# Two attentions keep program order on ScalarE and VectorE, gates close two pieces later, a memory tile is loaded apart from its square

## The chip, the cores and the metric

The kernel runs on one core of a Trainium2 chip. Five engines work side by side: TensorE (matmuls into PSUM banks; PE in the profile, its weight loads PEld), VectorE (DVE), ScalarE (ACT), GpSimd (POOL) and SyncE (SP), which here only issues DMAs. ScalarE and GpSimd issue DMAs too. Each engine takes its instructions from its own queue in a fixed order and waits on semaphores for the others. The metric is the device time of one execution in microseconds, the median of several runs.

## The reference

One layer of a decoder trunk, 1024 tokens of width 1024. Cut to what matters:

```python
h = rms_norm(x, norm1_g)
proj = h @ w_in                      # all branches' inputs and the gates
p_rwkv, p_sb, q_mem, gate_logits = split(proj)
y_a = rwkv7_branch(p_rwkv, ...)      # recurrence with a delta-rule state
y_b = stick_breaking_branch(p_sb)    # 8 heads of 64, causal, sigmoid weights and a reverse cumulative product
y_m = memory_branch(q_mem, mem, ...) # 4 heads of 128, softmax over 256 memory tokens
gates = sigmoid(gate_logits)         # 3 branches x 1024
x = x + sum_b(gates_b * (branch_b @ w_branch_b)) @ w_out
x = x + conv_ffn(rms_norm(x, norm2_g))
```

Everything is float32. A matmul that must be exact enough is made of three passes on TensorE's faster format: each operand is split into a high part and the rest.

## The kernel before, in words

The program is traced by Python in one order, and a planner then lays each engine's queue. The planner keeps its own clock: an instruction that by that clock has its inputs and its buffer is put into the queue, and one traced earlier that hasn't is passed by. So a queue's order can differ from the traced order. `pinned(ins)` (while `self.pin` is set) takes that freedom from one instruction: it comes behind the instruction traced just before it on the same engine, whatever that is. An instruction between two pinned ones that isn't pinned itself may still be put further ahead. Before the change all matmuls and transposes are pinned, and on VectorE the scans of the first attention and the triangular inverse.

TensorE's time is filled by weaving. A main generator (the first attention, then the second, then the recurrence) is run step by step, and after each step `weave` runs so many pieces of a filler, which is a stream of items. An item is mostly a projection: `proj_item` splits the weights (`split_raw`: a ScalarE copy, L80, and a GpSimd subtraction, L81; the split for an item is traced one item ahead), then does eight pieces k = 0 to 7 of six matmuls each into two PSUM banks (of the four with the tag `mm`), and then calls a `fin` that empties the banks. Extra work is hung on pieces by hooks.

- A gate item's `fin` copies the banks out (L745, ScalarE), multiplies by the row norms (L746, VectorE) and leaves a closure in `open_gates`. `close_gates`, called behind piece k = 2 of the next projection item, runs it: the sigmoid (L749) and a store of the gate to DRAM (L751, ScalarE's DMA queue). The gate's tile has the tag `w4`, of which there are three buffers; other items put their raw tiles and squares there too.
- First attention (`sb_attn`): 64 units of one head and 128 queries. `front` makes scores on TensorE and their sigmoid (L838, ScalarE); `weigh` scans (L844, VectorE, pinned); `mid`, two units later, transposes on TensorE (L105) and copies out (L856, ScalarE); `back`, for two units together, makes the weighted sums on TensorE, and then copies the heads out (L879) and stores them (L882, ScalarE's DMA queue). Scores and transposes share the four banks with the tag `g`. During it the fillers are the next heads' q and k projections, gates, and the memory's keys and values.
- Memory (`mem_kv`): `prep`, hung on piece 0 of one gate item and on piece 2 of another, loads 1024 columns of the memory tile (L909, SyncE's queue), squares it (L910) and splits it in four (L914 ScalarE, L915 VectorE). `ss` then sums the squares on TensorE.
- Second attention (`mem_attn`): eight units. `front` makes scores, their maximum (L1053, VectorE), a bias from it and the q norm's factor (L1056, VectorE; the factor comes from GpSimd, L697), exponentials (L1059, ScalarE), a reciprocal and a scaling (L1063, L1065); `mid` transposes and copies (L1074); `back` makes the sums and copies them out (L1084). The q projections are filler items; their `fin` is L1021 and L1022 on ScalarE and L1023 on VectorE.

The stage of the recurrence (`stage2`, about 800 to 1060 us) follows in the same manner, and then the output projection and the feed-forward network.

Of the kernel before, what the change touches and what calls it, by code (L numbers as in the profile page):

```python
# [11 lines left out]
F32 = mybir.dt.float32  # L12
F32R = mybir.dt.float32r
BF16 = mybir.dt.bfloat16
AF = mybir.ActivationFunctionType
ALU = mybir.AluOpType
AX = mybir.AxisListType
# [32 lines left out]
class Trunk:  # L50
# [649 lines left out]
    def proj_item(self, src, fin, hook={}):  # L700
        w = self.split_w(src)
        yield
        out = [self.ps("mm"), self.ps("mm")]
        for k in range(8):
            ks = slice(k * 128, (k + 1) * 128)
            self.mm3(out, [a[:, ks] for a in w], self.xin(k), k == 0, k == 7)
            if k == 2:
                self.close_gates()
            if k in hook:
                hook[k]()  # L710
            if k < 7:
                yield
        fin(out)
        yield
# [24 lines left out]
    def gate_item(self, b, d, hook={}, keep=None):  # L739
        nc = self.nc  # L740

        def fin(pp):
            g = self.t4()
            for h in range(2):
                nc.scalar.activation(g[:, h * 512 : (h + 1) * 512], pp[h], AF.Copy)  # L745
            nc.vector.tensor_tensor(g, g, self.rbc, ALU.mult)  # L746

            def close():
                nc.scalar.activation(g, g, AF.Sigmoid)  # L749
                if keep is None:  # L750
                    nc.scalar.dma_start(self.gsd[b, d], g)  # L751
                else:
                    keep["g", d] = g

            self.open_gates.append(close)

        return self.proj_item(self.I["w_in"][30 + b * 8 + d], fin, hook)
# [62 lines left out]
    def sb_attn(self, qk, need):  # L820
        nc = self.nc
        units = [(p, half, h2, half * 4 + bb) for p in range(4) for h2 in range(2) for half in range(2) for bb in range(4)]
        st = {}

        def front(u):
            p, half, h2, b = units[u]
            need(f"sb{p}")
            S, K, KL, nf = qk[p]
            W = (b + 1) * 128
            ts = slice(b * 128, (b + 1) * 128)  # L830
            sn = self.t4("at", n=1024)
            for w0 in range(0, W, 512):
                w1 = min(w0 + 512, W)
                pz = self.ps("g")
                self.mmul(pz[:, : w1 - w0], S[h2][:, ts], K[h2][:, w0:w1], start=True, stop=False)
                self.mmul(pz[:, : w1 - w0], S[h2][:, ts], KL[h2][:, w0:w1], start=False, stop=True)
                i = 2 * b + h2
                nc.scalar.activation(sn[:, w0:w1], pz[:, : w1 - w0], AF.Sigmoid, scale=nf[:, i : i + 1])  # L838
            st[u] = sn

        def weigh(u):
# [4 lines left out]
        def mid(u):  # L846
            b = units[u][3]
            W = (b + 1) * 128
            at, sn = self.t4("at"), st[u]
            st[u] = at  # L850
            for w0 in range(0, W, 512):
                w1 = min(w0 + 512, W)
                pt = self.ps("g")
                for o in range(w0, w1, 128):
                    self.transpose(pt[:, o - w0 : o - w0 + 128], sn[:, o : o + 128])
                nc.scalar.activation(at[:, w0:w1], pt[:, : w1 - w0], AF.Copy)  # L856

        def back(u):
            p, half, h2, b = units[u]
# [41 lines left out]
    def mem_kv(self):  # L901
        nc = self.nc
        mhi, mlo, sqs, st = [], [], [], {}

        def prep():
            i = len(sqs)
            raw, sq = self.t4(), self.t4()
            hi, lo = self.t4("qk", F32R), self.t4("qk", F32R)
            nc.sync.dma_start(raw, self.I["memT"][:, i * 1024 : (i + 1) * 1024])  # L909
            nc.scalar.activation(sq, raw, AF.Square)  # L910
            for kk in range(4):
                ks = slice(kk * 256, (kk + 1) * 256)
                g = self.par("memg", i * 4 + kk)
                nc.scalar.activation(hi[:, ks], raw[:, ks], AF.Copy, scale=g)  # L914
                nc.vector.scalar_tensor_tensor(lo[:, ks], raw[:, ks], g, hi[:, ks].bitcast(F32), ALU.mult, ALU.subtract)  # L915
            mhi.append(hi)
            mlo.append(lo)
            sqs.append(sq)
# [54 lines left out]
            self.mk = sq, kr, *st["r"]  # L973
            yield

        return prep, ss, [mv(i) for i in range(4)], [mk(h) for h in range(4)]

    def mem_kss(self):
        nc = self.nc
# [32 lines left out]
    def mem_q(self, h, out, hook):  # L1012
        nc = self.nc
        st = []

        def fin(pp):
            sq = self.t4()
            qhi, qlo = self.t4("qk", F32R), self.t4("qk", F32R)
            for i in range(2):
                hs = slice(i * 512, (i + 1) * 512)  # L1020
                nc.scalar.activation(qhi[:, hs], pp[i], AF.Copy, scale=self.par("memq"))  # L1021
                nc.scalar.activation(sq[:, hs], pp[i], AF.Square)  # L1022
                nc.vector.scalar_tensor_tensor(qlo[:, hs], pp[i], self.par("memq"), qhi[:, hs].bitcast(F32), ALU.mult, ALU.subtract)  # L1023
            st.extend((sq, qhi, qlo))

        def ss():
            sq, qhi, qlo = st
            pst = self.ps("g")
            for j in range(8):
                self.colsum(pst[:, j : j + 1], sq[:, j * 128 : (j + 1) * 128], self.ones[:, 0:1])  # L1030
            out.extend((qhi, qlo, self.head_norm(pst, 1, 128, 128 ** -0.5)))

        return self.proj_item(self.I["w_in"][26 + h], fin, hook), ss

    def mem_attn(self, mq, need):
        nc = self.nc
# [3 lines left out]
        def front(v):  # L1040
            h, i = units[v]
            need(f"mq{h}")
            qhi, qlo, f = mq[h]
            e = self.t4("at")
            sm = self.small("sm", [128, 4])
            for b2 in range(2):
                pz = self.ps("g")
                for u in range(2):
                    bs = slice((i * 4 + b2 * 2 + u) * 128, (i * 4 + b2 * 2 + u + 1) * 128)
                    self.mm3([pz[:, u * 256 : (u + 1) * 256]], [qhi[:, bs], qlo[:, bs]],  # L1050
                             [[kx[:, h * 256 : (h + 1) * 256]] for kx in self.kx], True, True)
                mxt = self.small("mxt", [128, 2])
                nc.vector.tensor_reduce(mxt, pz.rearrange("p (u m) -> p u m", u=2), AX.X, ALU.max)  # L1053
                fs = slice(i * 4 + b2 * 2, i * 4 + b2 * 2 + 2)
                nb = self.small("nb", [128, 2])
                nc.vector.scalar_tensor_tensor(nb, mxt, -1.0, f[:, fs], ALU.mult, ALU.mult)  # L1056
                for u in range(2):
                    o = (b2 * 2 + u) * 256
                    nc.scalar.activation(  # L1059
                        e[:, o : o + 256], pz[:, u * 256 : (u + 1) * 256], AF.Exp, bias=nb[:, u : u + 1],  # L1060
                        scale=f[:, fs.start + u : fs.start + u + 1], accum_out=sm[:, b2 * 2 + u : b2 * 2 + u + 1])
            rc = self.small("rc", [128, 4])
            nc.vector.reciprocal(rc, sm)  # L1063
            for b in range(4):
                nc.vector.tensor_scalar(e[:, b * 256 : (b + 1) * 256], e[:, b * 256 : (b + 1) * 256], rc[:, b : b + 1], None, ALU.mult)  # L1065
            es[v] = e

        def mid(v):
            e, pT = es[v], self.t4("at")
            for j in range(2):  # L1070
                pt = self.ps("g")
                for b in range(4):
                    self.transpose(pt[:, b * 128 : (b + 1) * 128], e[:, b * 256 + j * 128 : b * 256 + (j + 1) * 128])
                nc.scalar.activation(pT[:, j * 512 : (j + 1) * 512], pt, AF.Copy)  # L1074
            es[v] = pT

        def back(v):
            h, i = units[v]
            pT = es.pop(v)
            y = pT[:, 0:512]  # L1080
            py = self.ps("mm")
            for j in range(2):
                self.mmul(py, self.vm[:, j * 512 + h * 128 : j * 512 + (h + 1) * 128], pT[:, j * 512 : (j + 1) * 512], start=(j == 0), stop=(j == 1))
            nc.scalar.activation(y, py, AF.Copy)  # L1084
            nc.scalar.dma_start(self.yd[2, h, :, i * 512 : (i + 1) * 512], y)

        for s in range(len(units) + 4):
# [644 lines left out]
    def run(self):  # L1732
        nc, tc = self.nc, self.tc
# [26 lines left out]
        gate = lambda hook={}: self.gate_item(*gq.pop(0), hook)  # L1760
# [5 lines left out]
        mqi = [None] * 4  # L1766
        for h in range(4):
            mqi[h] = self.mem_q(h, mq[h], {2: mqi[h - 1][1], 4: mark(f"mq{h - 1}")} if h > 1 else {})
        items += [gate({0: prep}), gate(), gate({2: prep}), mss, *mv, *mk, mqi[0][0], mark("kv")]
        items += [self.mem_kss, gate({1: mqi[0][1]}), self.mem_kbc, mqi[1][0], mark("mq0")]  # L1770
        items += [mqi[2][0], mqi[3][0], gate({2: mqi[3][1], 4: mark("mq3")}), gate(), mark("mem")]
        ld1, br1 = self.branch(1, True)
# [114 lines left out]
```

## Time and profile before

| | us |
|---|---|
| median of 3 runs | 1866.93 |
| lowest, highest | 1861.88, 1868.17 |
| profiled execution | 1870.84 |
| its span | 1869.1 |
| first attention (ScalarE's first and last L838 to L879) | about 342 to 661 |
| second attention (its first maximum, its last store) | about 703 to 792 |

The page gives busy times by engine; the timeline gives instructions in order of time with, in brackets, how long the engine had been idle before and what ended the idle time. Names are tiles: `at<-g,nf` is written to a tile `at` from a bank `g` and a factor `nf`. L80, L105 and L112 are helpers (weight split, transpose, matmul), so their rows are told apart by their tiles: `mm<-xhi,wh` is a piece of a projection, `g<-qk,qk` scores of the first attention, `mm<-at,A` its weighted sums, `g<-kon,at` transposes, `g<-A,qk` scores of the second attention.

### The profile page before, as it was taken

How to read it: one execution, taken by the hardware profiler on the slowest of the kernel's cores; microseconds unless marked ns; L12 is line 12 of the kernel's file. 1: busy time of each engine (PE TensorE's matmuls, PEld its weight loads, DVE VectorE, ACT ScalarE, POOL GpSimd, SP SyncE). 2: the span in 40 equal slices, each digit the busy share in tenths (PEclk: the TensorE clock that was granted, in tenths of full speed). 3: DMA queues.
4: the chain of work that ended last, by engine and by line, in shares of the span. 5: the costliest groups of instructions: out<-in, count | busy, mean ns of one | idle time of the engine just before them, and what ended most of it. 6: DMA issues, size and time to landing. Idle time of an engine off the chain costs nothing. (4 is left out here: it accounts for less than half of the span.)

```text
span 1869.1 us, 27410 instructions
## 1 busy us (share of the span) xinstructions
PE 1801.6 (96%) x10468; PEld 1454.2 (78%) x10468; DVE 1169.7 (63%) x1654; ACT 884.8 (47%) x1667; POOL 785.7 (42%) x449
## 2 busy tenths in 40 slices
PE   8999999999999999999989999989999999999999
PEld 6777778878787787787767778767888888878877
DVE  5656665998887413333423673376777677785596
ACT  5443343565566535534446443454444444544333
POOL 2322343322222352122233352468676777644454
PEclk9999999999999999999899999999999999999999
DMA  4255465111122441557664472222333232486475
GB/s 177 57 169 180 158 208 177 51 61 43 40 63 65 121 128 40 171 207 260 231 218 170 157 260 91 102 79 95 114 107 108 85 119 97 134 303 221 141 235 193
DMA packets 120614, 263.39 MB, mean 141 GB/s; under 512 B 28314, under 2 KB 40858, under 8 KB 120355
## 3 DMA queue, kind: packets, MB, share of 16 engines
q1 hardware_dynamic: 82722, 194.76, 32.2%
q10 hardware_dynamic: 33984, 54.27, 7.9%
q0 software_dynamic: 3776, 12.62, 2.1%
q8 instruction: 82, 1.34, 0.3%
q14 instruction: 50, 0.40, 0.1%
HBM read 180.04 MB, written 81.53 MB: 140 GB/s over the span
## 5 line engine op out<-in xcount | busy, mean ns | idle before, releaser
L81 POOL TENSOR_TENSOR wl<-wr,wh 128x1024 fp32r<-128x1024 f32 x77 | 195.6, 2541 | 490.0 <-ACT wh L80 479.8
L112 PE MATMUL mm<-xhi,wh 128*128 128x512 f32 x784 | 267.8, 422 | 9.2 <-ACT xhi L179 7.4
L112 PE MATMUL mm<-xlo,wh 128*128 128x512 f32 x784 | 249.1, 400 | 0.8 <-DVE xlo L180 0.8
L112 PE MATMUL mm<-xhi,wl 128*128 128x512 f32 x784 | 246.2, 396 | 0.2 <-POOL wl L81 0.2
L112 PEld LDWEIGHTS mm<-xlo,wh 128*128 128x128 f32 x784 | 151.1, 193 | 35.4 <-DVE xlo L180 1.5
L112 PEld LDWEIGHTS mm<-xhi,wl 128*128 128x128 f32 x784 | 150.2, 192 | 34.6 <-POOL wl L81 0.6
L112 PEld LDWEIGHTS mm<-xhi,wh 128*128 128x128 f32 x784 | 139.7, 194 | 39.8 <-issue 9.1
L80 ACT ACTIVATE wh<-wr 128x1024 fp32r<-128x1024 f32 x77 | 81.4, 1057 | 146.2 <-PE mm L112 86.1
L112 PE MATMUL mm<-dw,da 128*128 128x512 f32 x528 | 121.6, 390 | 2.3 <-DVE da L1627 2.1
L112 PE MATMUL mm<-BT,l 128*128 128x512 f32 x504 | 118.0, 389 | 0.6 <-POOL l L1374 0.6
L112 PEld LDWEIGHTS mm<-dw,da 128*128 128x128 f32 x528 | 98.8, 188 | 24.4 <-DVE da L1627 3.4
L1628 POOL TENSOR_TENSOR dw<-draw,dw 128x512 fp32r<-128x512 f32 x55 | 81.3, 1487 | 83.5 <-ACT dw L1626 82.1
L844 DVE TENSOR_TENSOR_SCAN at<-at,at 128x128 f32<-128x128 f32 (+3 forms) x64 | 91.1, 1427 | 35.3 <-ACT at L838 35.2
L112 PEld LDWEIGHTS mm<-BT,l 128*128 128x128 f32 x504 | 94.5, 188 | 20.6 <-POOL l L1374 1.0
L112 PE MATMUL mm<-BT,wh 128*128 128x512 f32 x352 | 108.9, 390 | 0.7 <-DVE u L1426 0.7
L112 PE MATMUL mm<-B,wh 128*128 128x512 f32 x352 | 108.5, 389 | 0.0
L1627 DVE TENSOR_TENSOR da<-draw,da 128x512 fp32r<-128x512 f32 x77 | 65.7, 863 | 58.9 <-ACT da L1625 58.3
L112 PE MATMUL g<-dw,da 128*128 128x512 f32 x396 | 90.8, 390 | 2.1 <-POOL dw L1628 1.1
L1374 POOL TENSOR_TENSOR l<-it,l 128x1024 fp32r<-128x1024 f32 x21 | 50.8, 2419 | 92.3 <-ACT l L1373 92.3
L112 PEld LDWEIGHTS g<-dw,da 128*128 128x128 f32 x396 | 74.2, 188 | 18.2 <-ACT dw L1626 1.5
L1625 ACT ACTIVATE da<-draw 128x512 fp32r<-128x512 f32 x77 | 48.3, 628 | 83.1 <-PE mm L112 39.4
L746 DVE TENSOR_TENSOR w<-w,rbc 128x1024 f32<-128x1024 f32 x24 | 48.4, 2016 | 53.9 <-ACT w L745 53.9
(324 smaller groups left out, 4007.2 us busy)
## 6 DMA issues: line engine op xcount, KB each, us to landing
wr<-in_w_in_dram SPq DMA_DIRECT2D x50, 512.0 KB, 3.6
draw<-actd SPq DMA_DIRECT2D x77, 256.0 KB, 3.7
at<-scr SPq DMA_DIRECT2D x28, 512.0 KB, 6.0
draw<-in_w_down_dram SPq DMA_DIRECT2D x55, 256.0 KB, 4.6
wr<-in_w_up_dram SPq DMA_DIRECT2D x22, 512.0 KB, 3.5
actd<-gall ACTq DMA_DIRECT2D x44, 256.0 KB, 3.1
gsd<-w ACTq DMA_DIRECT2D x20, 512.0 KB, 2.8
rw<-in_w_up_dram SPq DMA_DIRECT2D x20, 512.0 KB, 3.6
```

Source lines behind the costliest of these rows:

```text
L80: self.nc.scalar.activation(hi, raw, AF.Copy)
L81: self.nc.gpsimd.tensor_tensor(lo, raw, hi.bitcast(F32), ALU.subtract)
L112: self.pinned(self.nc.tensor.matmul(*a, **k))
L746: nc.vector.tensor_tensor(g, g, self.rbc, ALU.mult)
L844: self.pinned(nc.vector.tensor_tensor_scan(sn[:, :W][:, ::-1], sn[:, :W][:, ::-1], self.smask[:, 1024 - W :][:, ::-1], 1.0, ALU.mult, ALU. ...
L1374: nc.gpsimd.tensor_tensor(lo, src, hi.bitcast(F32), ALU.subtract)
L1625: self.pinned(nc.scalar.activation(A[:, 0], a, AF.Copy))
L1627: self.pinned(nc.vector.tensor_tensor(A[:, 1], a, A[:, 0].bitcast(F32), ALU.subtract))
L1628: nc.gpsimd.tensor_tensor(Wt[:, 1], w, Wt[:, 0].bitcast(F32), ALU.subtract)
```

## The change

- In `proj_item` the gates are closed behind piece k = 4 instead of 2, and the gate's sigmoid (L749) is pinned.
- In `sb_attn` the scores' sigmoids (L838) and the copies of the transposes (L856) are pinned.
- In `mem_kv` the load of a memory tile becomes a function of its own, `load`. It is hung where `prep` was, on piece 0 and on piece 2; `prep` is hung on piece 5 and on piece 6 of the same items and takes only the square's and the splits' tiles. Its square (L910) and ScalarE splits (L914) are pinned; VectorE's (L915) aren't.
- In `mem_q` the three instructions of `fin` are pinned.
- In `mem_attn` all ScalarE and VectorE instructions are pinned.

Nothing that is computed changes, and no instruction is added or removed. Weight splits (L80), the copies of projections (L745 and the like) and the splits of keys and queries of the first attention stay unpinned.

```diff
@@ proj_item
-            if k == 2:
+            if k == 4:
                 self.close_gates()
@@ gate_item, close()
-                nc.scalar.activation(g, g, AF.Sigmoid)
+                self.pinned(nc.scalar.activation(g, g, AF.Sigmoid))
@@ sb_attn, front() and mid()
-                nc.scalar.activation(sn[:, w0:w1], pz[:, : w1 - w0], AF.Sigmoid, scale=nf[:, i : i + 1])
+                self.pinned(nc.scalar.activation(sn[:, w0:w1], pz[:, : w1 - w0], AF.Sigmoid, scale=nf[:, i : i + 1]))
-                nc.scalar.activation(at[:, w0:w1], pt[:, : w1 - w0], AF.Copy)
+                self.pinned(nc.scalar.activation(at[:, w0:w1], pt[:, : w1 - w0], AF.Copy))
@@ mem_kv
+        def load():
+            i = len(sqs)
+            st["raw"] = self.t4()
+            nc.sync.dma_start(st["raw"], self.I["memT"][:, i * 1024 : (i + 1) * 1024])
+
         def prep():
             i = len(sqs)
-            raw, sq = self.t4(), self.t4()
+            raw, sq = st.pop("raw"), self.t4()
             hi, lo = self.t4("qk", F32R), self.t4("qk", F32R)
-            nc.sync.dma_start(raw, self.I["memT"][:, i * 1024 : (i + 1) * 1024])
-            nc.scalar.activation(sq, raw, AF.Square)
+            self.pinned(nc.scalar.activation(sq, raw, AF.Square))
...
-                nc.scalar.activation(hi[:, ks], raw[:, ks], AF.Copy, scale=g)
+                self.pinned(nc.scalar.activation(hi[:, ks], raw[:, ks], AF.Copy, scale=g))
@@ mem_q, fin(): L1021, L1022 and L1023 pinned
@@ mem_attn: L1053, L1056, L1059, L1063, L1065, L1074 and L1084 pinned
@@ run
-        items += [gate({0: prep}), gate(), gate({2: prep}), mss, *mv, *mk, mqi[0][0], mark("kv")]
+        items += [gate({0: prep[0], 5: prep[1]}), gate(), gate({2: prep[0], 6: prep[1]}), mss, *mv, *mk, mqi[0][0], mark("kv")]
```

More of the change, by code (lines that the diff above doesn't have):

```diff
@@ L974, in mk @@
             yield
-        return prep, ss, [mv(i) for i in range(4)], [mk(h) for h in range(4)]
+        return (load, prep), ss, [mv(i) for i in range(4)], [mk(h) for h in range(4)]
     def mem_kss(self):
@@ L1020, in fin @@
                 hs = slice(i * 512, (i + 1) * 512)
-                nc.scalar.activation(qhi[:, hs], pp[i], AF.Copy, scale=self.par("memq"))
-                nc.scalar.activation(sq[:, hs], pp[i], AF.Square)
-                nc.vector.scalar_tensor_tensor(qlo[:, hs], pp[i], self.par("memq"), qhi[:, hs].bitcast(F32), ALU.mult, ALU.subtract)
+                self.pinned(nc.scalar.activation(qhi[:, hs], pp[i], AF.Copy, scale=self.par("memq")))
+                self.pinned(nc.scalar.activation(sq[:, hs], pp[i], AF.Square))
+                self.pinned(nc.vector.scalar_tensor_tensor(qlo[:, hs], pp[i], self.par("memq"), qhi[:, hs].bitcast(F32), ALU.mult, ALU.subtract))
             st.extend((sq, qhi, qlo))
@@ L1052, in front @@
                 mxt = self.small("mxt", [128, 2])
-                nc.vector.tensor_reduce(mxt, pz.rearrange("p (u m) -> p u m", u=2), AX.X, ALU.max)
+                self.pinned(nc.vector.tensor_reduce(mxt, pz.rearrange("p (u m) -> p u m", u=2), AX.X, ALU.max))
                 fs = slice(i * 4 + b2 * 2, i * 4 + b2 * 2 + 2)
                 nb = self.small("nb", [128, 2])
-                nc.vector.scalar_tensor_tensor(nb, mxt, -1.0, f[:, fs], ALU.mult, ALU.mult)
+                self.pinned(nc.vector.scalar_tensor_tensor(nb, mxt, -1.0, f[:, fs], ALU.mult, ALU.mult))
                 for u in range(2):
                     o = (b2 * 2 + u) * 256
-                    nc.scalar.activation(
+                    self.pinned(nc.scalar.activation(
                         e[:, o : o + 256], pz[:, u * 256 : (u + 1) * 256], AF.Exp, bias=nb[:, u : u + 1],
-                        scale=f[:, fs.start + u : fs.start + u + 1], accum_out=sm[:, b2 * 2 + u : b2 * 2 + u + 1])
+                        scale=f[:, fs.start + u : fs.start + u + 1], accum_out=sm[:, b2 * 2 + u : b2 * 2 + u + 1]))
             rc = self.small("rc", [128, 4])
-            nc.vector.reciprocal(rc, sm)
+            self.pinned(nc.vector.reciprocal(rc, sm))
             for b in range(4):
-                nc.vector.tensor_scalar(e[:, b * 256 : (b + 1) * 256], e[:, b * 256 : (b + 1) * 256], rc[:, b : b + 1], None, ALU.mult)
+                self.pinned(nc.vector.tensor_scalar(e[:, b * 256 : (b + 1) * 256], e[:, b * 256 : (b + 1) * 256], rc[:, b : b + 1], None, ALU.mult))
             es[v] = e
@@ L1073, in mid @@
                     self.transpose(pt[:, b * 128 : (b + 1) * 128], e[:, b * 256 + j * 128 : b * 256 + (j + 1) * 128])
-                nc.scalar.activation(pT[:, j * 512 : (j + 1) * 512], pt, AF.Copy)
+                self.pinned(nc.scalar.activation(pT[:, j * 512 : (j + 1) * 512], pt, AF.Copy))
             es[v] = pT
@@ L1083, in back @@
                 self.mmul(py, self.vm[:, j * 512 + h * 128 : j * 512 + (h + 1) * 128], pT[:, j * 512 : (j + 1) * 512], start=(j == 0), stop=(j == 1))
-            nc.scalar.activation(y, py, AF.Copy)
+            self.pinned(nc.scalar.activation(y, py, AF.Copy))
             nc.scalar.dma_start(self.yd[2, h, :, i * 512 : (i + 1) * 512], y)
```

## The prediction

> **What bounds the kernel now.** I read the page first: the span and the busy shares of the engines.
>
> ```profile
> span 1869.1 us, 27410 instructions
> PE 1801.6 (96%) x10468; PEld 1454.2 (78%) x10468; DVE 1169.7 (63%) x1654; ACT 884.8 (47%) x1667; POOL 785.7 (42%) x449
> ```
>
> TensorE is the bound: it is busy 96% of the span and idle for 67.5 us in all (1869.1 - 1801.6). Its matmuls stay as they are, in traced order. So the change can win only TensorE's waits in the stretches that it touches, and time at a lower clock. Next I took the groups of instructions for 340 to 760 us, the two attentions; behind the second bar stand the idle time ahead of a group and its releasers.
>
> ```profile
> L105 PE MATMUL g<-kon,at 128*128 128x128 f32 x320 | 47.1, 274 | 4.8 <-ACT at L856 3.7 <-DVE hn L691 1.0
> L749 ACT ACTIVATE w<-w 128x1024 f32<-128x1024 f32 x11 | 11.6, 1059 | 17.8 <-DVE w L746 17.8
> ```
>
> Most of the transposes' waiting there (3.7 of 4.8 us) ends with ScalarE's copies of transposed scores (L856), and ScalarE itself stood idle 17.8 us ahead of eleven gate sigmoids (L749), waiting for VectorE's product (L746). Then the windows around the longer waits. Columns: window, its length, busy time of PE, PEld, DVE, ACT and POOL, granted clock, DMA share, GB/s.
>
> ```profile
> 493.00:496.00 3.00, 0.20 (x3) 0.07 (x2) 2.93 (x4) 1.67 (x3) 0.00 (x0) 1.00 0.51 168
> 496.00:500.00 4.00, 4.00 (x13) 3.21 (x14) 3.97 (x6) 1.59 (x4) 0.00 (x0) 0.57 0.32 131
> 615.00:619.00 4.00, 1.51 (x20) 1.05 (x20) 1.08 (x2) 2.79 (x5) 0.00 (x0) 1.00 0.29 43
> 619.00:623.00 4.00, 4.00 (x25) 3.35 (x20) 0.46 (x1) 1.81 (x5) 0.00 (x0) 0.57 0.00 0
> 629.00:634.00 5.00, 5.00 (x25) 4.02 (x24) 4.23 (x4) 2.08 (x4) 4.60 (x3) 0.66 0.00 0
> 720.00:725.00 5.00, 2.12 (x12) 1.41 (x11) 1.82 (x5) 4.05 (x12) 2.61 (x2) 1.00 0.40 96
> 725.00:729.00 4.00, 4.00 (x14) 3.37 (x14) 2.53 (x8) 2.21 (x7) 0.00 (x0) 0.57 0.13 45
> 884.00:900.00 16.00, 11.57 (x78) 8.48 (x72) 7.57 (x21) 7.20 (x25) 5.85 (x3) 0.68 0.78 277
> 948.00:962.00 14.00, 8.14 (x49) 6.10 (x49) 4.18 (x20) 1.74 (x8) 4.71 (x3) 0.76 0.55 191
> ```
>
> Each of the three waits at 493, 615 and 720 us is followed by 4 us in which TensorE is fully busy, but at a granted clock of 0.57. Such a window loses 4.00 x (1 - 0.57) = 1.72 us more.
>
> **The change part by part.** First, the gate's sigmoid: pinned, and closed behind piece k = 4 instead of k = 2. The timeline of the first wait shows what it does today (start, duration, what, and in brackets the wait before it):
>
> ```profile
> 486.17 0.38 ACT L856 ACTIVATE at<-g 128x256 f32<-128x256 f32 x1
> 486.96 1.53 PE L112 MATMUL mm<-at,A 128*64 128x128 f32 x22
> 489.81 3.23 DVE L807 SCALAR_TENSOR_TENSOR qk<-w,params,qk 64x1024 fp32r<-64x1024 f32 x1
> 493.08 1.22 DVE L746 TENSOR_TENSOR w<-w,rbc 128x1024 f32<-128x1024 f32 x1
> 494.33 1.06 ACT L749 ACTIVATE w<-w 128x1024 f32<-128x1024 f32 x1 [5.02 <-DVE w L746]
> 495.30 0.58 ACT L856 ACTIVATE at<-g 128x512 f32<-128x512 f32 x1
> 495.93 0.66 PE L105 MATMUL g<-kon,at 128*128 128x128 f32 x4 [2.80 <-ACT at L856]
> 496.34 1.02 PE L112 MATMUL mm<-xhi,wh 128*128 128x512 f32 x2
> ```
>
> The sigmoid's place in the program is behind the item's third piece, which starts at 496.34. It ran at 494.33, so it had been put ahead, into ScalarE's queue in front of copies traced earlier, and there it stood 5.02 us for a product that VectorE reached late (behind the 3.23 us split). The copies came out at 495.30 and TensorE waited 2.80. Pinned and two pieces later, the sigmoid comes behind those copies, and its product is done when ScalarE gets to it. I take the 2.80 as gone, and the 0.94 of a second case, below. What is late next is VectorE, busy 2.93 of 3 and 3.97 of 4 us there, but the transposes that waited asked for a copy, not for it.
>
> The price: sigmoid and store issue (1.06 and, below, 0.33, together 1.39) now lie in front of copies traced behind k = 4. The least cushion I see is 0.41: a copy ends at 486.17 + 0.38 = 486.55 and the weighted sums start at 486.96. So one gate costs between 0 and 1.39 - 0.41 = 0.98, and eleven between 0 and 10.8. ScalarE is idle about half the time, so I take 0.5 for all. Queued behind a waiting sigmoid are its store, on ScalarE's DMA queue, and the pinned copies.
>
> Second, the memory tile: its load traced on its own, its square and splits five and four pieces later and pinned.
>
> ```profile
> 572.72 1.06 ACT L749 ACTIVATE w<-w 128x1024 f32<-128x1024 f32 x1 [3.15 <-DVE w L746]
> 574.17 1.05 ACT L910 ACTIVATE w<-w 128x1024 f32<-128x1024 f32 x1
> 574.32 0.66 PE L105 MATMUL g<-kon,at 128*128 128x128 f32 x4 [0.94 <-ACT at L856]
> 575.11 1.70 ACT L914 ACTIVATE qk<-w,params 128x256 fp32r<-128x256 f32 x4
> 609.77 0.70 PE L112 MATMUL mm<-xhi,wh 128*128 128x512 f32 x2
> 610.09 0.33 ACTq L751 DMA_DIRECT2D gsd<-w  x1
> 610.35 0.42 DVE L844 TENSOR_TENSOR_SCAN at<-at,at 128x128 f32<-128x128 f32 x1 [0.56 <-ACT at L838]
> 612.27 0.71 PE L112 MATMUL mm<-xhi,wh 128*128 128x512 f32 x2
> 615.79 1.06 ACT L910 ACTIVATE w<-w 128x1024 f32<-128x1024 f32 x1 [3.16 <-DMA gsd<-w]
> 618.14 2.48 PE L112 MATMUL mm<-at,A 128*64 128x128 f32 x28 [2.48 <-ACT at L856]
> 621.93 0.45 ACTq L882 DMA_DIRECT2D yd<-ys  x1
> 623.42 0.27 PE L105 MATMUL g<-kon,at 128*128 128x128 f32 x1
> ```
>
> The second square (615.79) blocked ScalarE for 3.16 us until the gate's store had left the buffer that the square writes: store issued at 610.09, landed by 615.79, so 5.7 us. Copies queued behind it made TensorE wait 2.48. After the change the gate closes behind k = 4 and the square comes behind k = 6, two pieces on; a piece with the attention's work between takes 612.27 - 609.77 = 2.50, so 5.0 us lie between and the copies' time besides: the store has landed or nearly so. I take the 2.48 as gone; the other end is 0.7 of it (5.7 - 5.0). The price: square and four splits are 1.05 + 1.70 = 2.75 us in one go, now in front of copies that run 0.41 or more ahead; at 574.17 the same burst cost TensorE nothing. Between 0 and 2 x 2.34, I take 0.6. The two loads go to SyncE's queue at the traced place that they have now; the raw tile only takes its buffer apart from the square's, so no queue passes another: 0. The gate's buffer, one of three, stays taken for two pieces more. Its next user comes at the item's end, three pieces (7.5 us) behind the close, and 1.39 + 5.7 = 7.1 suffice even with that slow store: 0, at most the 3.16 of one such wait.
>
> Third, the pins on the first attention's sigmoids (L838) and copies (L856). They already run in traced order but for one thing: a score's sigmoid no longer passes the store issue of the finished heads (0.45, sixteen times: 0 to 7.2). The sigmoid's result goes to a scan, and from a scan's end to its transposes there is room: 610.35 + 0.42 to 623.42, 12.65 us there, of which the wait made 2.48. So 0.
>
> Fourth, the second attention and its q projections.
>
> ```profile
> 713.81 0.21 POOL L697 TENSOR_TENSOR hf<-hf,rsc 128x8 f32<-128x8 f32 x1
> 716.17 1.28 DVE L1053 TENSOR_REDUCE mxt<-g 128x2 f32<-128x512 f32 x2
> 718.33 1.06 ACT L80 ACTIVATE wh<-wr 128x1024 fp32r<-128x1024 f32 x1 [3.47 <-issue]
> 720.49 0.75 DVE L1023 SCALAR_TENSOR_TENSOR qk<-mm,params,qk 128x512 fp32r<-128x512 f32 x1 [3.04 <-ACT w L1022]
> 722.22 0.22 DVE L1056 SCALAR_TENSOR_TENSOR nb<-mxt,hf 128x2 f32<-128x2 f32 x2
> 722.46 0.56 ACT L1059 ACTIVATE at<-g,nb,hf 128x256 f32<-128x256 f32 x1 [0.95 <-DVE nb L1056]
> 723.72 2.40 PE L112 MATMUL g<-A,qk 128*128 128x256 f32 x12 [2.77 <-ACT at L1059]
> ```
>
> The scores' maxima end at 717.45 and their factor was ready at 714.02, yet the bias (L1056) ran at 722.22: VectorE's queue held the projection's splits (L1023) in front of it, which waited for the projection's end. The exponentials came 5 us late and TensorE waited 2.77 for their banks. Pinned, L1056 runs at about 717.5. ScalarE's weight split (L80) isn't pinned and may stay ahead: then two exponentials end at 718.33 + 1.06 + 2 x 0.56 = 720.5, and TensorE asks at 723.72 - 2.77 = 720.95. So the 2.77 goes; between 0 and 2.77 may stay, I take 0.5 for all fronts.
>
> The sum: waits 2.80 + 0.94 + 2.48 + 2.77 = 8.99; clock 3 x 1.72 = 5.16; new costs 0.5 + 0.6 + 0.5 = 1.6. Together 8.99 + 5.16 - 1.6 = 12.55 us less. The profiled execution took 1870.84 (span 1869.1 and 1.74 around it), so 1858.3; that execution lies 3.91 above the median of the runs, 1866.93, so in the runs 1854.4.
>
> [...]
>
> **The rivals.**
>
> Waits go, clock stays: the windows at low clock come from the stage's thin matmuls, as the one at 629 us, with no wait before it, suggests. Then 8.99 - 1.6 = 7.4 less: 1859.5. Against it: the waits and the three windows stand in pairs.
>
> Slower: ScalarE's order becomes TensorE's. Place: the copies that run only 0.41 us ahead of their sums. Price: 0.98 for a gate and 1.72 if the clock drops behind it, so 2.70; for all eleven 29.7, less the 14.15 won: 15.6 slower, 1882.5. It decides from the sixth gate on (6 x 2.70 = 16.2). Against it: ScalarE has idle time ahead of most of these copies.
>
> Later stage re-ordered: the chain's stage (800 to 1060 us) isn't pinned, and its order is planned anew behind the change. It holds two stalls, each of idle and clock: 16.00 - 11.57 + 0.32 x 16.00 = 9.55, and 14.00 - 8.14 + 0.24 x 14.00 = 9.22. One more such stall leaves 12.55 - 9.4 = 3.2 less, 1863.8, about no change; one fewer gives 1845.0.
>
> The change does nothing: the unpinned weight splits still go ahead and hold the same copies. Then 1866.9. Against it: the wait of each of the four rows names the sigmoid, the square or the splits that are now pinned.
>
> **How the numbers follow.** 0.3% of 1866.93 is 5.6 us; less than that can hardly be told from no change here. The sum's case 0.60 (its own range 1848 to 1862: all new costs at nothing and the window at 629 us won too, 5.00 x 0.34 = 1.70, or one wait with its window kept, with some 3 us for the spread of the runs); clock stays 0.10; slower 0.15; later stage 0.10, half each way; nothing 0.05. Faster: nearly all of the first, most of the second, half of the fourth: 0.72. Same: 0.12. Slower: 0.16. The range of 1846 to 1870 leaves out most of the slower case and the best of the fourth, together under 0.2.
>
> **What would show it.** Right: L749 no longer waits for L746 in the attentions; no row of L105 or L112 with a wait over 1 us for L856 at the four places; L910 without a wait for a store; L1056 ahead of L1023; the clock at 1.00 where it was 0.57; TensorE's idle time in the two attentions down by 8 to 9 us. Wrong: new waits of L112 on L856 behind a gate's close, a square that still waits for the store, or the stall moved to the stage behind 800 us.

## The result and the profile after

The changed kernel takes 1852.94 us (median of six runs, 1851.25 to 1855.63), the kernel before 1866.9 us in the runs beside it (1861.88 to 1870.62). The ratio is 0.993, 95% interval 0.9918 to 0.9943: 0.6 to 0.8% faster. The forecast was 1854.4 us. The profiled execution took 1854.88 us against 1870.84 before. Two executions on record, 2580.69 us of the kernel before and 2962.27 of an experiment, ran at mean granted clocks of 0.643 and 0.556 and are left out of every ratio.

The first lines of the page of the changed kernel:

```profile
span 1853.1 us, 27444 instructions
PE 1793.0 (97%) x10468; PEld 1448.0 (78%) x10468; DVE 1171.0 (63%) x1654; ACT 880.9 (48%) x1665; POOL 783.6 (42%) x449
```

The span is 16.0 us shorter. TensorE's idle time fell from 67.5 to 1853.1 - 1793.0 = 60.1, so by 7.4; its busy time fell by 8.6, with the same 10468 matmuls. (The 34 instructions more are 36 more semaphore operations and two loads fewer of ScalarE's function tables, 12 instead of 14.) A matmul at half clock counts as busy for longer (before, `mm<-xhi,wl` took 628 ns each between 496.56 and 499.97 us, at a clock of 0.50, and 397 between 500.00 and 503.30, at 1.00), so the second number should be the clock. The view of the cores gives a mean granted clock of 0.987 before and 0.992 after. The clock that was not granted is 0.013 x 1869.1 = 24.3 us before and 0.008 x 1853.1 = 14.8 us after: 9.5 less, where one step of the rounded clock is 1.9 us. So in this pair of executions about half of the gain is waits and half is clock. Other executions differ in the clock's part, as shown below. Where the gain lies, by windows over both attentions, before (290 to 800 us) and after (290 to 790):

```profile
290.00:800.00 510.00, 496.59 (x3235) 404.24 (x3234) 325.43 (x366) 277.13 (x515) 145.54 (x79) 0.98 0.28 86
```
```profile
290.00:790.00 500.00, 494.45 (x3259) 403.81 (x3258) 328.65 (x368) 276.29 (x517) 147.44 (x80) 1.00 0.29 90
```

TensorE idles 510.00 - 496.59 = 13.41 us there before and 500.00 - 494.45 = 5.55 after: 7.86 less, so all of the idle time that was won was won in the attentions. The two groups of 340 to 760 us that the prediction began with now read:

```profile
L105 PE MATMUL g<-kon,at 128*128 128x128 f32 x336 | 48.5, 273 | 1.9 <-DVE hn L691 1.1 <-DVE at L844 0.7
L749 ACT ACTIVATE w<-w 128x1024 f32<-128x1024 f32 x11 | 11.6, 1059 | 2.6 <-DVE w L746 2.6
```

The gate's sigmoids wait 2.6 us instead of 17.8, and what is left of the transposes' waiting is no longer for ScalarE's copies (L856). The memory tile's squares, L914 now, wait for no store either (0.0 us idle ahead of both). The windows at the places of the three long waits (now 493, 612 and 706 us), and at the two stalls of the chain's stage:

```profile
493.00:496.00 3.00, 2.26 (x15) 1.88 (x15) 3.00 (x3) 1.56 (x4) 0.00 (x0) 1.00 0.46 161
496.00:500.00 4.00, 4.00 (x28) 3.15 (x27) 3.93 (x6) 0.95 (x1) 0.00 (x0) 1.00 0.32 131
612.00:616.00 4.00, 4.00 (x28) 3.28 (x25) 0.89 (x1) 2.73 (x7) 0.00 (x0) 1.00 0.16 37
706.00:711.00 5.00, 5.00 (x30) 4.21 (x28) 1.52 (x5) 3.25 (x10) 2.11 (x1) 1.00 0.03 7
868.00:886.00 18.00, 13.13 (x106) 10.06 (x101) 9.22 (x23) 9.34 (x32) 5.85 (x3) 0.81 0.76 266
932.00:946.00 14.00, 8.70 (x55) 6.54 (x53) 4.18 (x20) 1.74 (x8) 4.55 (x3) 0.76 0.46 167
```

TensorE is busy throughout at 612 and 706, waits 0.74 at 493, and the clock is 1.00 in all four rows of the attentions. The chain's stage keeps both stalls. The timeline shows the order that does it:

```profile
493.96 1.19 DVE L746 TENSOR_TENSOR w<-w,rbc 128x1024 f32<-128x1024 f32 x1
494.19 1.06 PE L105 MATMUL g<-kon,at 128*128 128x128 f32 x8 [0.74 <-DVE at L844]
494.91 1.09 ACT L856 ACTIVATE at<-g 128x512 f32<-128x512 f32 x2 [0.90 <-PE g L105]
495.88 1.06 ACT L749 ACTIVATE w<-w 128x1024 f32<-128x1024 f32 x1
...
707.50 0.16 DVE L1060 SCALAR_TENSOR_TENSOR nb<-mxt,hf 128x2 f32<-128x2 f32 x1
707.75 1.06 ACT L80 ACTIVATE wh<-wr 128x1024 fp32r<-128x1024 f32 x1 [3.13 <-issue]
708.71 0.55 ACT L1063 ACTIVATE at<-g,nb,hf 128x256 f32<-128x256 f32 x1
712.58 1.40 DVE L1027 SCALAR_TENSOR_TENSOR qk<-mm,params,qk 128x512 fp32r<-128x512 f32 x2
```

The sigmoid (L749) now follows the copies (L856) and waits for nothing. The bias of the exponentials (L1060, L1056 before) runs 5 us ahead of the projection's splits (L1027, L1023 before). The unpinned weight split (L80) still goes in front of the exponentials, as the prediction allowed, and costs TensorE nothing.

### The profile page after: what moved, and what is told of

The parts are those of the page before. It is cut to its first block, busy times and chain, and to the rows that moved or that the text cites. A ratio compares the mean times of both kernels' runs of the same rounds, so it can differ in the third digit from the quotient of the medians.

```text
span 1853.1 us, 27444 instructions
## 1 busy us (share of the span) xinstructions
PE 1793.0 (97%) x10468; PEld 1448.0 (78%) x10468; DVE 1171.0 (63%) x1654; ACT 880.9 (48%) x1665; POOL 783.6 (42%) x449
## 5 line engine op out<-in xcount | busy, mean ns | idle before, releaser
L80 ACT ACTIVATE wh<-wr 128x1024 fp32r<-128x1024 f32 x77 | 81.4, 1057 | 144.6 <-PE mm L112 85.5
L112 PEld LDWEIGHTS mm<-dw,da 128*128 128x128 f32 x528 | 98.8, 188 | 24.3 <-DVE da L1631 3.4
L844 DVE TENSOR_TENSOR_SCAN at<-at,at 128x128 f32<-128x128 f32 (+3 forms) x64 | 93.3, 1459 | 26.6 <-ACT at L838 26.4
```

Source lines behind the costliest of these rows:

```text
L80: self.nc.scalar.activation(hi, raw, AF.Copy)
L112: self.pinned(self.nc.tensor.matmul(*a, **k))
L844: self.pinned(nc.vector.tensor_tensor_scan(sn[:, :W][:, ::-1], sn[:, :W][:, ::-1], self.smask[:, 1024 - W :][:, ::-1], 1.0, ALU.mult, ALU. ...
```

## The experiments

The theory: TensorE's waits came from operations put ahead in ScalarE's and VectorE's queues, and each long wait costs itself and a stretch at half clock. First, each part of the change was made alone, in the kernel before. All ratios are to the kernel before, with 95% intervals; 0.001 is 1.9 us.

**The gates' part alone.**

```diff
-            if k == 2:
+            if k == 4:
                 self.close_gates()
-                nc.scalar.activation(g, g, AF.Sigmoid)
+                self.pinned(nc.scalar.activation(g, g, AF.Sigmoid))
```

> The kernel before with the gates' part alone: sigmoid pinned and closed behind piece 4. Theory (a wait costs itself and the half-clock window behind it, and each part removes its own): the waits at 493 and 573 us go, 2.80 + 0.94, and the window behind the first, 1.72, less 0.5 of new cost: 5.0 us less, a ratio of 0.9973; the waits at 615 and 720 us stay, with their windows. Rival (the clock does not follow the wait): 3.74 - 0.5 = 3.2 less, and a window at 496 us with TensorE fully busy at 0.57. Rival (the pins hold copies up): new TensorE waits behind the closes, no gain.

Measured: 0.9952 (0.9934 to 0.9971), 9.0 us less where 5.0 were expected. The wait of 2.80 us at 493 went and left one of 0.74, for a scan (L844); the one at 573 went, and the one at 615 us, which I had put down to the memory tile's part, went as well. The 2.77 us before the second attention's scores stayed.

**The memory tile's part alone.** The load becomes a function of its own and stays where it was; the square and splits are pinned and come later.

```diff
-        items += [gate({0: prep}), gate(), gate({2: prep}), mss, ...
+        items += [gate({0: prep[0], 5: prep[1]}), gate(), gate({2: prep[0], 6: prep[1]}), mss, ...
```

> The kernel before with the memory tile's part alone: load split off, square and splits five and four pieces later and pinned. Theory: the wait at 615 us goes, 2.48, with the window behind it, 1.72, less 0.6: 3.6 us less, a ratio of 0.9981; the window at 629 us (1.70), which had no wait before it, goes as well if it belongs to the wait at 615, 5.3 less then. Rival (the clock does not follow the wait): 1.9 less. The gates' sigmoids still go ahead of copies, so the wait at 493 us stays.

Measured: 0.998 (0.9969 to 0.9991), 3.7 us less. The wait at 615 us went, those at 493 and 573 stayed. But the clock did not do as the theory said. A window at half clock stood at 624 us with no wait ahead of it, and none behind the wait of 2.77 us that ended at 717.38, in the second of these rows:

```profile
712.78:716.19 3.41, 1.84 (x11) 1.25 (x9) 1.64 (x4) 2.46 (x6) 3.05 (x2) 1.00 0.00 0
716.19:719.60 3.41, 2.10 (x14) 1.86 (x15) 1.11 (x5) 3.21 (x10) 0.09 (x1) 1.00 0.75 193
719.60:723.02 3.42, 3.42 (x42) 2.70 (x42) 1.60 (x5) 1.82 (x7) 0.00 (x0) 1.00 0.00 0
```

**The second attention's part alone** (the pins in mem_q and mem_attn).

> The kernel before with the second attention's and its q projections' pins alone. Theory: the wait at 720 us goes, 2.77, with the window behind it, 1.72, less 0.5: 4.0 us less, a ratio of 0.9979; L1056 runs right behind its maximum, ahead of the splits L1023. Rival (the clock does not follow the wait): 2.3 less. Rival (the weight split on ScalarE holds the exponentials up all the same): under 1 us less.

Measured: 0.9974 (0.9962 to 0.9985), 4.9 us less. The wait at 720 us went, the others stayed. Ten lines were pinned at once, so which of them it takes isn't shown.

**The first attention's pins alone.**

```diff
-                nc.scalar.activation(sn[:, w0:w1], pz[:, : w1 - w0], AF.Sigmoid, scale=nf[:, i : i + 1])
+                self.pinned(nc.scalar.activation(sn[:, w0:w1], pz[:, : w1 - w0], AF.Sigmoid, scale=nf[:, i : i + 1]))
...
-                nc.scalar.activation(at[:, w0:w1], pt[:, : w1 - w0], AF.Copy)
+                self.pinned(nc.scalar.activation(at[:, w0:w1], pt[:, : w1 - w0], AF.Copy))
```

> The kernel before with the pins on the first attention's sigmoids (L838) and copies (L856) alone. Theory: they run in traced order already but for the store issue: nothing, a ratio of 0.999 to 1.001, and all four waits (493, 573, 615, 720 us) stay. Rival (these pins are what keeps the copies in front of the sigmoid and the square): the waits at 493 and 615 us go here already, 5.3 us less and 3.4 for their windows.

Measured: 1.0015 (1.0004 to 1.0026), 2.8 us more. The four waits stayed and one grew, from 0.94 to 3.44 us. The timeline of this kernel:

```profile
571.42 1.06 ACT L749 ACTIVATE w<-w 128x1024 f32<-128x1024 f32 x1 [3.12 <-DVE w L746]
572.39 1.04 ACT L910 ACTIVATE w<-w 128x1024 f32<-128x1024 f32 x1
573.33 1.69 ACT L914 ACTIVATE qk<-w,params 128x256 fp32r<-128x256 f32 x4
574.93 0.95 ACT L856 ACTIVATE at<-g 128x512 f32<-128x512 f32 x2
575.56 0.66 PE L105 MATMUL g<-kon,at 128*128 128x128 f32 x4 [3.44 <-ACT at L856]
```

Before, the copies that these transposes waited for stood between sigmoid and square. Pinned, they come behind square and splits as well, 2.7 us later. Pinning only the operations that are overtaken leaves those that overtake them free.

The gates' and the second attention's parts alone give 9.0 + 4.9 = 13.9 us, as much as the whole change; the memory tile's part took away a wait that the gates' part takes away too. Next, which half of the gates' part it is, and what the other two are worth beside them.

**The gates' pin alone, closed behind piece 2 as before.**

> The kernel before with the gates' sigmoid pinned alone, still closed behind piece 2. If the pin carries the gates' part: the sigmoid comes behind the copies that it stood in front of, the waits at 493 and 573 us go, and since the gate's part alone took 9.0 us off (0.9952, with the wait at 615 us gone too), this takes most of it: 0.996 or lower. If the two pieces are needed as well: the sigmoid in traced order comes before VectorE has its product, ScalarE waits in order and TensorE's waits stay or move, 0.998 to 1.001.

Measured: 0.9946 (0.9932 to 0.996), 10.1 us less: all of the gates' part. The groups of 340 to 760 us, and the timeline at the place of the former wait at 615:

```profile
L749 ACT ACTIVATE w<-w 128x1024 f32<-128x1024 f32 x11 | 11.7, 1062 | 3.6 <-DVE w L746 3.6
L910 ACT ACTIVATE w<-w 128x1024 f32<-128x1024 f32 x2 | 2.1, 1056 | 4.0 <-DMA gsd<-w 4.0
```
```profile
604.24 0.33 ACTq L751 DMA_DIRECT2D gsd<-w  x1
607.78 1.97 PE L112 MATMUL mm<-at,A 128*64 128x128 f32 x30
610.01 1.06 ACT L910 ACTIVATE w<-w 128x1024 f32<-128x1024 f32 x1 [3.95 <-DMA gsd<-w]
```

The square (L910) still waits 3.95 us for the gate's store, longer than before, and TensorE waits for nothing: the copies that it needs (L856, ended at 606.06) are now in front of the square. ScalarE's wait was not the price by itself; what stood behind it was.

**Closed behind piece 4, without the pin.**

> The kernel before with the gates closed behind piece 4 alone, nothing pinned. If the pin carries the gates' part: the sigmoid is still put ahead of copies traced earlier, the wait at 493 us stays; 0.998 to 1.001. If the two pieces carry it: 0.996 or lower, with the waits at 493 and 573 us gone.

Measured: 0.9984 (0.9974 to 0.9993), 3.0 us less. The waits at 493 and 573 us stayed (2.80 and 0.91), as with the sigmoid still put ahead; the one at 615 went. So three different edits alone take that wait away.

**The changed kernel without the first attention's pins.**

> The changed kernel without the pins on the first attention's sigmoids and copies (L838, L856). Alone these pins made it 0.15% slower, by a sigmoid and a square that were put in front of copies which could no longer move. In the changed kernel sigmoid and square are pinned too. If the loss was that: the same as the changed kernel, 0.993 +- 0.001. If these pins cost by themselves: 2.8 us less, 0.9915. If they are needed beside the others: waits of TensorE for L856 come back, 0.994 or more.

Measured: 0.9924 (0.9912 to 0.9937), the same as the changed kernel within the intervals. With sigmoid and square pinned, these pins neither cost nor bring anything that can be told.

**The changed kernel without the memory tile's part.**

> The changed kernel without the memory tile's part (load, square and splits in one piece at the old places, not pinned). The gates' part alone already took the wait at 615 us away. If the two do the same thing twice: the same as the changed kernel, 0.993 +- 0.001. If the memory tile's part is needed: the wait at 615 us (2.5) comes back, with or without a window at half clock behind it, 2.5 to 4.2 us more, 0.9945 to 0.9955.

Measured: 0.9931 (0.9918 to 0.9943), the same. No wait came back at 615 us.

**The gates' pin and the second attention's pins, nothing else.**

> The kernel before with two of the edits alone: the gates' sigmoid pinned (still behind piece 2), and the second attention's and its q projections' pins. Alone they gave 0.9946 and 0.9974. If these two are all that the change is worth: 0.992 to 0.993, the same as the changed kernel, with no wait over 2 us left in the two attentions. If the later sigmoid, the memory tile's part or the first attention's pins add something beside them: 0.994 or more, with a wait at about 490, 570 or 615 us.

Measured: 0.9933 (0.9919 to 0.9946), the same as the whole change; no wait over 1.2 us is left in the two attentions. The transposes between 340 and 760 us:

```profile
L105 PE MATMUL g<-kon,at 128*128 128x128 f32 x336 | 48.7, 273 | 1.1 <-DVE hn L691 1.0
```

The 0.74 us at 493 us isn't there either. All seven profiled kernels with the sigmoid pinned and closed behind piece 4 have it (0.72 to 0.74), the two with the pin alone don't. So of the five edits (the sigmoid's pin, the closing behind piece 4, the first attention's pins, the memory tile's part, the second attention's pins) two do all that can be told.

**What sets the clock.** The half-clock windows in each profile start on a grid of 3.41 us, at a phase that differs from execution to execution: 496.56, 619.44 and 725.25 us before lie 36 and 31 steps apart, and 876.43 us after lies 111.3 steps behind the first of them. Put on its own grid, the kernel before shows at the wait of 493 us

```profile
493.14:496.56 3.42, 0.63 (x5) 0.63 (x6) 3.35 (x4) 2.23 (x5) 0.00 (x0) 1.00 0.53 183
496.56:499.97 3.41, 3.41 (x10) 2.62 (x9) 3.41 (x5) 1.03 (x3) 0.00 (x0) 0.50 0.28 114
```

one stretch with 2.79 us idle, and the next at 0.50 from end to end; at the wait of 2.77 us, 1.99 of which fall into one stretch (721.84 to 725.25), the same. In the memory tile's kernel the grid cuts the wait of 2.77 us into 1.57 and 1.31 (the three rows above), and the clock stays. In the kernel with the first attention's pins it cuts 3.44 us:

```profile
570.62:574.03 3.41, 1.49 (x10) 1.12 (x8) 1.47 (x3) 2.61 (x4) 0.00 (x0) 1.00 0.71 245
574.03:577.44 3.41, 1.88 (x10) 1.63 (x11) 3.41 (x9) 3.18 (x8) 0.00 (x0) 1.00 0.16 65
```

1.92 and 1.53 us idle, no half clock. So the clock went with the idle time within one stretch: 1.99 us and more were followed by half clock here, 1.92 us and less were not. The bound isn't sharp. Over all stretches at full clock in the fourteen profiles (behind the first 10 us, and without matmuls of fewer than 64 columns), 1.95 us idle or more was followed by half clock in 76 of 76, 1.6 to 1.95 us in 10 of 36, less than that once in 6957. In a stretch that was itself at half clock less was enough: with 0.43 us idle or more the next was at half clock as well, 40 of 40. So one wait cost two stretches: with the gates' pin alone the one of 2.76 us (2.17 in one stretch, 0.60 in the next) brought 6.83 us at 0.50.

The window without a wait (629 us before) should then come from work that counts as idle: the 64 matmuls of a single column that sum the memory tile's squares. To test that, they were issued twice over.

```diff
-            for j in range(2):
+            for j in [0, 1, 0, 1]:
                 for k in range(8):
                     o = (k % 4) * 256 + j * 128
                     self.colsum(pst[:, j : j + 1], sqs[k // 4][:, o : o + 128], self.ones[:, 0:1], k == 0, k == 7)
```

> The changed kernel with the 64 matmuls of one column behind the memory tile's squares issued twice over (32 sums for each column of the factors; the second pass writes the same values again). They take 2.03 us of TensorE, in the kernel before at 626 us with a half-clock window behind them though TensorE waited for nothing. If the clock is set by how much of a fixed 3.41 us stretch TensorE spends idle or on such thin matmuls (from the six profiles so far: 1.6 us and less never brings a half-clock stretch next, 2.0 us and more always): 4.06 us of them fill at least 2.03 us of one stretch wherever the grid lies, so a window at half clock follows for certain; 2.0 + 1.7 = 3.7 us more than the changed kernel, ratio 0.995. If only waits lower the clock: no window, 2.0 us more, 0.994.

Measured: 0.9955 (0.9943 to 0.9966), 4.7 us more than the changed kernel. The sums and the grid around them:

```profile
618.18 5.24 PE L112 MATMUL g<-kon,w 128*64 128x1 f32 x128
```
```profile
616.92:620.34 3.42, 3.42 (x80) 2.92 (x80) 2.69 (x5) 3.42 (x8) 0.00 (x0) 1.00 0.01 2
620.34:623.75 3.41, 3.41 (x65) 3.41 (x64) 0.30 (x2) 0.29 (x1) 0.05 (x1) 0.50 0.02 5
623.75:627.16 3.41, 3.41 (x12) 2.60 (x11) 2.80 (x2) 0.95 (x2) 3.41 (x2) 0.50 0.00 0
```

TensorE is busy in every row, and two stretches run at half clock, one more than expected. The rival, no window, is out. But "2.0 us and more always" was too strong for these matmuls. The changed kernel has its 64, 2.03 us, within one stretch too:

```profile
617.02:620.43 3.41, 3.41 (x75) 2.87 (x74) 2.66 (x6) 2.33 (x6) 0.00 (x0) 1.00 0.00 0
620.43:623.85 3.42, 3.42 (x19) 2.78 (x18) 3.02 (x2) 2.65 (x5) 2.73 (x2) 1.00 0.00 0
```

and the next stretch is at full clock. Of seven profiles with all 64 in one stretch, half clock followed in two (before and the memory tile's part alone); with them issued twice, 2.16 us of them between 616.92 and 620.34 brought it. So in these profiles single-column matmuls went with the clock as idle time does, or nearly so, and 2.03 us of them lie at the bound.

**The chain's stage.** Its two stalls were left by the change, and they look alike. In the changed kernel:

```profile
873.26 1.06 ACT L1108 ACTIVATE yhi<-w 128x1024 fp32r<-128x1024 f32 x1 [3.58 <-DMA w<-yd]
874.34 0.92 ACT L547 ACTIVATE qk<-g 64x64 f32<-64x64 f32 x4
874.84 0.81 PE L112 MATMUL g<-ys,at 64*64 64x64 f32 x8 [3.11 <-ACT qk L547]
...
936.90 2.54 DVE L582 TENSOR_SCALAR qk<-qk,hn,hf 128x64 f32<-128x64 f32 x11 [7.20 <-POOL hf L166]
939.36 0.61 DVE L527 COPY ys<-g 128x64 f32<-128x64 f32 x4
939.63 1.12 PE L112 MATMUL g<-ys,qk 64*64 64x64 f32 x16 [5.30 <-DVE ys L527]
```

Twice an operation that waits stands in front of the chain's copies. First the norm's scalings were moved two steps on, and they, the copies L527 and the updates L545 pinned:

```diff
         self.rsqrt(rs[:, : 4 * nh], vs[:, : 4 * nh], 4 * nh, 1.0 / 64, 64e-5)
         yield
+        yield
+        yield
...
-                nc.vector.tensor_scalar(y, y, nm[:, j : j + 1], rs[:, j : j + 1], ALU.add, ALU.mult)
+                self.pinned(nc.vector.tensor_scalar(y, y, nm[:, j : j + 1], rs[:, j : j + 1], ALU.add, ALU.mult))
```

> The changed kernel, and in the chain's stage the same remedy: VectorE's copies and updates of the chain (L527, L545) and the norm's scalings (L582) pinned in program order, the scalings two steps later, behind the norm's factor. In the changed kernel a scaling that waited 7.2 us for that factor stood in front of the copies L527, and TensorE waited 5.30 us at 934 us, with two half-clock windows behind. If that order is the cause: the wait goes, 5.3 and up to 3.4 us less than the changed kernel, ratio to the kernel before 0.988 to 0.990. If the factor itself (from GpSimd) is what the chain needs: the wait stays, 0.993.

Measured: 0.9965 (0.9952 to 0.9978), slower than the changed kernel. The 5.30 us went, and the other stall grew from 3.11 to 13.64:

```profile
881.13 2.26 ACT L1110 ACTIVATE yhi<-w 128x1024 fp32r<-128x1024 f32 x2 [4.11 <-DMA w<-yd]
882.22 2.43 DVE L1111 TENSOR_TENSOR A<-w,yhi 128x1024 fp32r<-128x1024 f32 x2 [4.99 <-ACT yhi L1110]
884.57 0.85 DVE L545 SCALAR_TENSOR_TENSOR ys<-ys,pc,g 128x64 f32<-128x64 f32 x4
885.38 1.90 PE L112 MATMUL g<-ys,at 64*64 64x64 f32 x16 [13.64 <-ACT qk L547]
```

The pinned update L545 now stood behind the splits of the next branch's input (the last two, L1110 and L1111, are in the rows), which waited for their loads: the first attention's lesson again. Then the loads were taken out of the way as well, each tile into the buffer of its low part, the splits one by one in the gate that follows:

```diff
+    def load_y_early(self, b, ys):
+        self.yraw = [self.t4("A", F32R) for _ in range(4)]
+        hi = self.pool_a.tile([128, 4, 1024], F32R, name=self.nm("yhi"), tag="inst")
+        for k, t in enumerate(self.yraw):
+            self.nc.sync.dma_start(t.bitcast(F32), self.yd[b, k])
+            ys.append((hi[:, k], t))
...
-        ... ld2, gate(), *br2, ...
+        ... ld2, gate({k + 3: self.ysplit(k) for k in range(4)}), *br2, ...
```

> The kernel of e_norm, and the four tiles of the next branch's input loaded ahead in one go, each into its low part's own buffer, and split one by one behind pieces 3 to 6 of the gate that follows, pinned. In the changed kernel such a split (L1108) waited 3.6 us on ScalarE for its load with the chain's copies (L547) behind it, and TensorE waited 3.11, 0.82 and 0.80 us from 872 us on, with two half-clock windows behind. If the order is the cause: 4.7 and up to 3.4 us less than e_norm, ratio 0.984 to 0.987. If the loads come too late for their buffers all the same: TensorE waits for the splits at the next branch, same as e_norm or slower.

Measured: 1849.1 us, 0.9908 (0.9896 to 0.9921), 4.1 us less than the changed kernel by the two ratios, whose intervals just touch; all its runs (1847.16 to 1850.24) lie below the changed kernel's (from 1851.25). Both stalls are gone, but less was won than expected. The profiled span is 7.7 us shorter than the changed kernel's, and the traces show where. The 1850 matmuls that take the changed kernel 217.29 us, from 851 us on, take 209.46 here. TensorE's idle time among them falls by 5.37, from 14.38 to 9.01, though the four waits named were 10.0: the rest came back in shorter waits, the longest 2.32. No half-clock window is left there, which is 6.83 us of lost clock less, but its busy time falls by 2.46 only. Why the busy time at full clock grew by 4.4 us isn't settled.

## Why the prediction was right, and where not

**The waits, 8.99.** Right in sum: the idle time of the attentions fell by 7.86 net of all new waits, and all four waits are gone. The attribution was wrong in one step, "the memory tile". That part alone does take its 2.48 away, but so does the gates' pin alone, and beside that pin the part is worth nothing that can be told. I had looked for five us to let the store land before the square; the square may wait for it once the copies are in front.

**Two pieces later.** I counted on them for the product to be done when ScalarE gets to the sigmoid. Not needed: at piece 2, pinned, the sigmoids wait 3.6 us in all and TensorE not at all for the copies behind them. With the pin, piece 4 even comes with the 0.74 us at 493 us that piece 2 doesn't have.

**The first attention's pins, 0.** Right beside the other edits. Alone they cost 2.8 us, a case that the prediction did not see because the change holds all of them at once.

**The clock, 5.16.** The size of one stretch, 1.72, was right (3.41 us at half clock, 1.71); that each wait has exactly one was not. The profiled execution of before happened to have one behind each of the three and the one at 629 us; the profiled one after had none in the attentions behind 320 us. What counts for the medians is the mean over executions, and the record has it: each run's span times the share of the clock that it wasn't granted. Over 62 executions of the kernel before this is 20.0 us in the mean, over the six of the changed kernel 14.2, so 5.8 less with a standard error of 1.1. With the 15 runs of the three kernels that measured the same it is 15.1, so 5.0 less, standard error 0.6. The term of 5.16 agrees with both. The grid alone makes it a little less: as an estimate from the bounds of 1.95 and 0.43, a wait of 2.8 brings one stretch in (3.41 - (2 x 1.95 - 2.8)) / 3.41 = 0.68 of its positions and a second in (2.8 - 0.43 - 1.95) / 3.41 = 0.12, and three such waits cost 3 x 0.80 x 1.71 = 4.1. The rival that the clock stays fell, but its argument, the window without a wait, was sound: 2.03 us of thin matmuls alone brought one, in two of seven profiles.

**The price, 1.6.** Nearly of the right size. Without new waits 13.41 - 8.99 = 4.42 us would be left; 5.55 are, so 1.13 came: 0.74 at 493 us, for a scan on VectorE and not for the copies that I named, and 0.39 in small pieces. That the size is near is luck: the largest piece is of a kind that I had not priced. The head-of-line mechanism of the slower rival did not appear in the changed kernel, and did in two of the experiments, where only one side of an order was pinned.

**The later stage.** Neither better nor worse in order: both stalls stayed, 18.00 - 13.13 = 4.87 and 14.00 - 8.70 = 5.30 us of idle time.

**The sum.** 12.55 less was forecast; 14.0 less by the medians, 13.1 by the ratio. Both halves of the sum hold by themselves: waits net of new ones, 8.99 - 1.6 = 7.4 forecast and 7.86 in the profiles; clock, 5.16 forecast and 5.0 to 5.8 over the runs.

## What to carry to other kernels

Where an engine that is half idle makes the bounding engine wait, look in its queue for what stands in front of the operation waited for; fix the order of the one that goes ahead, and not of the one that is overtaken. An operation may wait when nothing urgent is queued behind it, so a long wait on such an engine is no price by itself (the square's 3.95 us, with the gates' pin alone, cost TensorE nothing). Try each edit of a bundle alone and left out: here two of five did all the work that can be told.

## What was unexpected of the hardware

In these profiles half clock came in stretches of 3.41 us on a fixed grid, after a stretch in which TensorE was idle, or ran single-column matmuls, for somewhat over half the time (1.95 us idle or more in 76 of 76, 2.03 us of such matmuls in two of seven); 2.79 us in one stretch did it, 3.44 us cut in two did not.

And a scan of 1024 columns on VectorE and a subtraction of GpSimd's, which overlap in time, ended as if run one after the other. The 0.74 us at 493 us waited for this scan. The rows are of the changed kernel, and then of the kernel before at the same place:

```profile
488.56 3.33 POOL L81 TENSOR_TENSOR wl<-wr,wh 128x1024 fp32r<-128x1024 f32 x1 [1.22 <-ACT wh L80]
489.67 4.38 DVE L844 TENSOR_TENSOR_SCAN at<-at,at 128x1024 f32<-128x1024 f32 x1
```
```profile
487.50 2.28 DVE L844 TENSOR_TENSOR_SCAN at<-at,at 128x1024 f32<-128x1024 f32 x1
487.80 4.16 POOL L81 TENSOR_TENSOR wl<-wr,wh 128x1024 fp32r<-128x1024 f32 x1 [1.22 <-ACT wh L80]
```

Whichever started second ended some 2.2 us behind the first: the scan at 494.05 behind 491.89 in the changed kernel, the subtraction at 491.96 behind 489.78 before, where the scan, being first, took no longer than elsewhere (2.29 us at 598.93). All fourteen profiles show this pair in one of the two forms. So in these rows the scan took 2.28 us where it started first and 4.38 where it started second, both with GpSimd running beside it. What delays the second isn't shown.
